# A hybrid decoder layer: the mLSTM's matmuls as three rounded passes, the local branch's weights rounded by casting transfers, and the gate rows' transpositions moved

## The chip, the cores and the metric

The kernel runs on one core of a Trainium2 chip. A core has a matrix engine (TensorE, PE), a vector engine (VectorE, DVE), a scalar engine (ScalarE, ACT), a general engine (GpSimd, POOL) and a synchronisation engine (SyncE, SP); SP and POOL issue most of the DMA transfers, each through a queue of its own. Every engine works through its own instructions in a fixed order and waits on semaphores where an input or a buffer isn't ready. On-chip memory has a large part (SBUF), with 128 partitions, and a small one (PSUM), into which PE writes its products.

The metric is the device time of one execution in microseconds (us), as a median of several executions.

## The reference

One decoder layer on a sequence of 512 tokens with 1024 channels. A normalised input feeds an mLSTM branch (4 heads, q and k of 128, v of 256 channels) and a sliding-window attention branch (16 query heads, 4 key heads of 64, window 128, with sinks). Each branch is multiplied by its weights and a sigmoid gate; the sum goes through an output projection, then come an MLP with squared ReLU, a gated per-layer embedding and a last norm. Everything is float32. Cut to the branches:

```python
proj = rmsnorm(x, norm_mix_g) @ w_in
qk_ml, v_ml, o_ml, if_pre, q_sw, k_sw, v_sw, g_a, g_b = split(proj)
qk_ml = silu(causal_depthwise_conv(qk_ml, conv_qk))
h_ml = mlstm_chunkwise(q_ml * ML_DQK ** -0.5, k_ml, v_ml, ig, lf)
h_ml = h_ml * rsqrt(mean(h_ml * h_ml) + EPS)
y_a = sigmoid(o_ml) * h_ml * mlstm_norm_g
y_b = swa_with_sinks(q_sw, k_sw, v_sw, sinks)
merged = sigmoid(g_a) * (y_a @ w_branch_a) + sigmoid(g_b) * (y_b @ w_branch_b)
x = x + merged @ w_out
```

The kernel computes the mLSTM without chunks, over the whole 512 x 512 lower triangle: for a head, scores k·q are multiplied by exp(log decay), and the result by v. The denominator is a row sum of the same weighted scores, which comes out of the same product through a column of ones beside v.

## The kernel before

**Arithmetic.** Most products are made of three passes in a rounded float32 format (F32R). An operand is split into a high part, the value rounded by a cast on ACT, and a low part, the rest, by a subtraction on DVE (`split`, L134). A product is then high·high + high·low + low·high (`pairs` L163, `chain` L169). Two products of the mLSTM are an exception: the scores (L819) and the output (L831) are plain float32 matmuls.

**Weights.** `load_w` (L155) loads 512 KB of weights through SP's queue into a raw buffer `wr` and splits it into `wh` and `wl`, each with four buffers (`WB`).

**v and the output gate.** `by_tokens` (L484) makes v (`w_vml`) and then the output gate (`w_o`) by seven half-size products instead of eight, through `seven` (L438): sums of weight quadrants are formed on DVE (L448 to L462), and the seven products are named p1, c11, t21, t22, c22, c12, c21. Each of them is two half products (one for each of two weight tiles) of 12 passes with 512 columns, 14 half products in all. p1 and c11 share a pair of PSUM banks (`pst`), so c11's first half product, the third of the 14, may start only when p1 has been copied out on ACT (L507); the first half product of t21, the fifth, writes another pair (`psg`). `put_v` (L517) writes v into the tiles `vm`, `put_o` (L582) takes the sigmoid and sends the gate to device memory (`god`).

**Gate rows.** Input and forget gates are made into rows of 4 x 512 on DVE (`mst`, a scan; `rr`, `gg`), and `em` is an exponential of `mst` on ACT (L562), whose table has to be loaded first. Between v and the output gate, 14 small transpositions on PE (L572, L574) turn `gg` and `em` into columns, and five DVE copies (L577, L578) bring them into `gc`.

**mLSTM and the local branch's weights.** After the attention come: the last q and k projection (`qk_proj(7)`), all eight SiLUs, then a loop over the four heads. Per head there are `ml_decay` (exponentials on ACT), `ml_scores`, `ml_out`, and one product of the local branch, `branch_b` (24 passes with 512 columns, eight of them in all), as work for PE while the other engines prepare the next head. The other four `branch_b` stand between the transpositions of the heads' results (`ya_of`).

**Order.** Each engine's order is set when the program is built: a scheduler places instructions from their dependences and program order; `issue_after` keeps a group behind a named matmul. Buffers are handed round in rings, so an instruction also waits for the last reader of the buffer that it writes.

Of the kernel before, what the change touches and what calls it, by code (L numbers as in the profile page):

```python
# [16 lines left out]
P = 128  # L17
# [19 lines left out]
def block_kernel(  # L37
# [82 lines left out]
    def tk(n):  # L120
        return tp_.tile([P, NH * (DV + 1)], F32, tag="tk", bufs=4, name=nm(n))

# [6 lines left out]
    def r32(t):  # L129
        return t.bitcast(F32)  # L130
# [348 lines left out]
    for m in range(NT):  # L479
        t = tk("vm").rearrange("p (h d) -> p h d", h=NH)  # L480
        G.memset(t[:, :, DV : DV + 1], 1.0)
        vm.append(t)

    def by_tokens(w, post, own_first=False):  # L484
# [81 lines left out]

    pgc = pg[:, :512]
    with tc.issue_after(last_mm[0].ins):
        for t in range(NT):
            for s in range(t + 1):  # L570
                c = (t * NT + s) * 4
                T.transpose(pgc[:, c : c + 4], gg[t][:, s * P : (s + 1) * P], ident[:4, :4])  # L572
            c = (NT * NT + t) * 4
            T.transpose(pgc[:, c : c + 4], em[:, t * P : (t + 1) * P], ident[:4, :4])  # L574
    gc = c1.tile([P, NT * NT + NT, 4], F32, name="gc")
    for t in range(NT):
        V.tensor_copy(gc[:, t * NT : t * NT + t + 1, :], pgc[:, t * NT * 4 : (t * NT + t + 1) * 4].rearrange("p (a b) -> p a b", b=4))  # L577
    V.tensor_copy(gc[:, NT * NT :, :], pgc[:, NT * NT * 4 : (NT * NT + NT) * 4].rearrange("p (a b) -> p a b", b=4))  # L578


    god = dp.tile([P, NH, NT, DV], F32, name="god")
# [9 lines left out]

    by_tokens(w_o, post_by_tokens(put_o))

# [178 lines left out]

    qk_proj(7)

    for h in range(NH):
        silu(h)
        silu(4 + h)


    hs = [[act_f("hs") for _ in range(2)] for _ in range(NH)]  # L780
# [7 lines left out]
    def ml_decay(h):  # L788
# [7 lines left out]
        )  # L796
        wT = []
        for s in range(NT):
            dm = act_f("dm")
            for t in range(s, NT):  # L800
                src = dg if t == s else pr
                A.activation(
                    dm[:, t * P : (t + 1) * P],
                    src[:, t * P : (t + 1) * P],
                    AF.Exp,
                    bias=gc[:, t * NT + s, h : h + 1],
                )
            wT.append(dm)
        wts[h] = wT

    def ml_scores(h):

        two, one = ps_a(), ps_t()
        banks = [two[:, :512], two[:, 512:], one, two[:, 512:]]
        at = [0, 0, 0, 384]
        for s in (0, 1, 3, 2):
            n0 = s * P
            psc = banks[s][:, at[s] : at[s] + S - n0]
            T.matmul(psc, qk[4 + h][:, n0 : n0 + P], qk[h][:, n0:], start=True, stop=True, skip_group_check=True)  # L819
        for s in range(NT):  # L820
            n0 = s * P
            dm = wts[h][s]
            V.tensor_mul(dm[:, n0:], banks[s][:, at[s] : at[s] + S - n0], dm[:, n0:])

    def ml_out(h):
        wT = wts.pop(h)
        for half in (1, 0):
            pn = ps_a().rearrange("p (n c) -> p n c", n=2)
            for t in (2 * half, 2 * half + 1):
                for s in range(t + 1):  # L830
                    last_mm[0] = T.matmul(  # L831
                        pn[:, t % 2, : DV + 1], wT[s][:, t * P : (t + 1) * P], vm[s][:, h, :], start=s == 0, stop=s == t, skip_group_check=True
                    )
            A.copy(hs[h][half].rearrange("p (n c) -> p n c", n=2), pn[:, :, :DV])
            V.tensor_copy(hd[:, h, 2 * half : 2 * half + 2], pn[:, :, DV])
# [24 lines left out]
    def branch_b(i):  # L860
        ps = ps_g()
        mm_T(ps, load_w(w_b[i], KT * P, KT), yb)
        t2[i] = act_f("gb")
        V.tensor_mul(t2[i], ps, gate_of(gbd, i))


    _, ya = big_hl("ya")

# [6 lines left out]

    ml_decay(0)
    ml_scores(0)
    rds = []
    for h in range(NH):
# [12 lines left out]
    for h in range(NH):  # L892
        branch_b(NH + h)
        ya_of(h)


# [541 lines left out]
```

## Time and profile before

| | |
|---|---|
| median of three runs | 880.56 us (880.06 to 881.1) |
| the profiled execution | 879.82 us, of which 878.0 us span |
| mean clock granted to PE | 0.998 |
| output gate's half products | from 83.45 us |
| mLSTM with the local branch's products | about 325 to 399.55 us |

The span is what the profile covers, from its first instruction to its last; the rest of an execution lies around it. The profile's page gives busy shares of the engines and the chain of waits that ended last; the views by window and the timeline of one engine show a stretch of the program. Names such as `psg<-x,wh` mean that a tile `psg` was written from `x` and `wh`; L171 is the line of the kernel. The lines themselves stand in the prediction, where they are used.

### The profile page before, as it was taken

The page shows a single profiled execution, that of the slowest core. Times are in us where ns is not written, and L with a number is a line of the kernel's source. Part 1 is how long each engine was busy: PE and PEld are TensorE (multiplying, and loading weights), DVE is VectorE, ACT ScalarE, POOL GpSimd, SP SyncE. Part 2 cuts the span into 40 slices and gives each one's busy share as a digit, 9 for nine tenths or more (in the row PEclk, how much of TensorE's full clock was granted, in tenths as well). Part 3 has the DMA queues.
Part 4 walks back from the last instruction along what each step waited for, and adds up shares of the span by engine and source line. Part 5 has one row for each costly group of instructions (what it writes and reads, how often), then busy time and mean ns, then how long its engine had stood idle before and what let it go on. Part 6 is the DMA issues. An engine that isn't in the chain of part 4 may idle for free.

```text
span 878.0 us, 11545 instructions
## 1 busy us (share of the span) xinstructions
PE 866.8 (99%) x4372; PEld 725.6 (83%) x4372; DVE 657.2 (75%) x966; ACT 483.5 (55%) x803; POOL 34.1 (4%) x58
## 2 busy tenths in 40 slices
PE   8999999999999999999999999999999999999996
PEld 7888889998777777788888888888888888888886
DVE  6999887875789876665896669756956794698557
ACT  6684554544676768743344665356435634564843
POOL 1111010000000000000020000000000000020000
PEclk9999999999999999999999999999999999999999
DMA  7765244435122162274244612530352054125302
GB/s 266 211 180 186 73 150 169 165 111 196 52 73 72 49 199 88 97 240 144 72 75 145 236 49 71 197 106 10 124 185 75 1 186 149 49 52 141 121 0 96
DMA packets 32793, 106.74 MB, mean 122 GB/s; under 512 B 4573, under 2 KB 4573, under 8 KB 32738
## 3 DMA queue, kind: packets, MB, share of 16 engines
q1 hardware_dynamic: 27570, 93.15, 31.2%
q0 software_dynamic: 5024, 12.59, 5.9%
q8 instruction: 34, 0.56, 0.3%
q10 hardware_dynamic: 144, 0.26, 0.1%
q14 instruction: 21, 0.17, 0.1%
HBM read 91.30 MB, written 8.40 MB: 114 GB/s over the span
## 4 chain that ended last, share of the span: by engine, by line
PE 90%; DVE 4%; ACT 3%; DMA 2%; issue 1%; SPq 0%; ACTq 0%; DVEq 0%
PE psg L171 50%; PE psp L171 23%; PE psa L171 7%; PE pst L171 4%; PE psa L831 1%; PE pst L747 1%; DVE wl L138 1%; DMA wr<-in_w_vsif 1%; ACT lm L712 1%; PE psa L819 1%; PE psa L689 1%; PE psa L690 1%; ACT wh L137 0%; DMA wr<-in_w_gb 0%; PE psp L980 0%
## 5 line engine op out<-in xcount | busy, mean ns | idle before, releaser
L137 ACT CAST wh<-wr 128x1024 fp32r<-128x1024 f32 x138 | 144.8, 1051 | 180.3 <-PE psg L171 74.8
L138 DVE TENSOR_TENSOR wl<-wr,wh 128x1024 fp32r<-128x1024 f32 x138 | 167.8, 1219 | 85.9 <-ACT wh L137 84.6
L171 PE MATMUL psg<-x,wh 128*128 128x512 f32 x512 | 157.7, 389 | 0.0
L171 PE MATMUL psp<-wh,uf 128*128 128x512 f32 x448 | 138.6, 389 | 0.0
L171 PEld LDWEIGHTS psg<-x,wh 128*128 128x128 f32 x512 | 96.0, 188 | 19.9
L171 PE MATMUL psg<-x,wl 128*128 128x512 f32 x256 | 99.6, 389 | 0.0
L171 PEld LDWEIGHTS psp<-wh,uf 128*128 128x128 f32 x448 | 84.1, 188 | 17.5
L171 PE MATMUL psp<-wl,uf 128*128 128x512 f32 x224 | 87.2, 389 | 0.0
L171 PE MATMUL psg<-h,wh 128*128 128x512 f32 x256 | 81.1, 395 | 0.7 <-DVE rc L715 0.7
L137 ACT CAST wh<-wd 128x1024 fp32r<-128x1024 f32 x44 | 46.2, 1052 | 54.0 <-PE psp L171 21.9
L138 DVE TENSOR_TENSOR wl<-wd,wh 128x1024 fp32r<-128x1024 f32 x44 | 53.1, 1217 | 14.7 <-ACT wh L137 14.5
L171 PEld LDWEIGHTS psg<-x,wl 128*128 128x128 f32 x256 | 48.0, 188 | 10.0
L171 PEld LDWEIGHTS psg<-h,wh 128*128 128x128 f32 x256 | 47.0, 188 | 11.2 <-issue 1.6
L171 PE MATMUL psg<-h,wl 128*128 128x512 f32 x128 | 50.5, 395 | 0.0
L138 DVE TENSOR_TENSOR uf<-F,uf 128x1792 fp32r<-128x1792 f32 (+2 forms) x20 | 33.0, 1652 | 21.8 <-ACT uf L137 21.8
L171 PEld LDWEIGHTS psp<-wl,uf 128*128 128x128 f32 x224 | 42.0, 188 | 8.7
L171 PE MATMUL psg<-yb,wh 128*128 128x512 f32 x128 | 41.3, 402 | 0.1
L171 PE MATMUL psg<-ya,wh 128*128 128x512 f32 x128 | 39.5, 390 | 0.0
L137 ACT CAST uf<-F 128x1792 fp32r<-128x1792 f32 (+2 forms) x20 | 27.9, 1396 | 20.5 <-DVE F L1133 20.4
L1157 DVE SCALAR_TENSOR_TENSOR xk<-psp,r,xk 128x512 f32<-128x512 f32 x48 | 33.7, 744 | 5.5 <-PE psp L171 5.2
L171 PE MATMUL psg<-hS,wh 128*128 128x256 f32 x192 | 35.6, 284 | 0.0
L171 PE MATMUL psa<-h,wh 128*128 128x256 f32 x192 | 35.3, 285 | 0.2 <-ACT p L625 0.2
(322 smaller groups left out, 1745.6 us busy)
## 6 DMA issues: line engine op xcount, KB each, us to landing
wr<-in_w_up SPq DMA_DIRECT2D x32, 512.0 KB, 3.3
wd<-in_w_down SPq DMA_DIRECT2D x24, 512.0 KB, 3.7
wr<-in_w_qsw SPq DMA_DIRECT2D x8, 512.0 KB, 4.3
gd<-gr POOLq DMA_DIRECT2D x8, 512.0 KB, 3.7
wr<-in_w_qkml SPq DMA_DIRECT2D x8, 512.0 KB, 3.2
wr<-in_w_b SPq DMA_DIRECT2D x8, 512.0 KB, 3.2
gl<-gd SPq DMA_DIRECT2D x8, 512.0 KB, 3.4
wr<-in_w_a SPq DMA_DIRECT2D x8, 512.0 KB, 4.4
```

What stands on the lines that cost most here:

```text
L137: A.copy(dst[0], src)
L138: last_low[0] = V.tensor_sub(dst[1], src, r32(dst[0]))
L171: last_mm[0] = T.matmul(ps, l, r, start=first and i == 0, stop=last and i == len(ops) - 1, skip_group_check=parts)
L689: T.matmul(o, q[:, n * P : (n + 1) * P], kk[kp][ab][:, k0 : k0 + 256], start=True, stop=False)
L690: T.matmul(o, q[:, n * P : (n + 1) * P], kl[kp][ab][:, k0 : k0 + 256], start=False, stop=True)
L712: A.activation(lm3[:, g, :], lm3[:, g, :], AF.Exp, bias=nmx[:, g : g + 1], scale=0.125, accum_out=sm[:, g : g + 1])
L747: T.matmul(o[HALF[ab], :], v[:, c : c + 64], w[:, ab * 512 : (ab + 1) * 512], start=j == 0, stop=j == len(terms) - 1)
L819: T.matmul(psc, qk[4 + h][:, n0 : n0 + P], qk[h][:, n0:], start=True, stop=True, skip_group_check=True)
L831: last_mm[0] = T.matmul(pn[:, t % 2, : DV + 1], wT[s][:, t * P : (t + 1) * P], vm[s][:, h, :], start=s == 0, stop=s == t, skip_group_check ...
L1157: V.scalar_tensor_tensor(o, ps[:, t, :], r2[:, 2 * toks + t : 2 * toks + t + 1], o, ALU.mult, ALU.add)
```

## The change

1. The mLSTM's scores and output become three rounded passes each. q and k of a head are split (`qk_parts`), as are the weighted scores (in pieces of 512, 384 and 384 columns), into tiles of `ya`, which isn't needed until later. The score pieces are kept without their empty left parts: for the last two key blocks both products have 256 columns.
2. v is stored rounded in `vm`, with two columns of ones a head. Its low part is made by a subtraction and sent to device memory (`vld`, eight writes through POOL's queue); `ml_out` reads it back (`vl`, 512 KB a head through SP's queue).
3. `branch_b`'s weights get their high part by a transfer from device memory that casts (POOL's queue) instead of the cast on ACT; the low part is still a subtraction on DVE, from the raw tile that SP's queue loads as before.
4. The gate rows' transpositions and the copies into `gc` move from before the output gate to after its product t21.
5. In the mLSTM stage `ml_decay(0)` and the buffers come ahead of `qk_proj(7)`; only head 0's SiLUs and split stand before the first scores; two `branch_b` stand before head 0's output, one before each later one, a further one before head 3's scores, and two instead of four are left for the transpositions of the results.

```diff
-    def load_w(src, n, dims, raw=None):
+    def load_w(src, n, dims, raw=None, cast=False):
...
-        split(parts, raw[:, :n])
+        if cast:
+            nc.gpsimd.dma_start(out=parts[0], in_=src)
+            last_low[0] = V.tensor_sub(parts[1], raw[:, :n], r32(parts[0]))
+        else:
+            split(parts, raw[:, :n])
...
     def put_v(m, nh, ps, k):
         o = vm[m][:, 2 * nh : 2 * nh + 2, :DV]
-        src = ps.rearrange("p (h d) -> p h d", h=2)
+        two = lambda t: t.rearrange("p (h d) -> p h d", h=2)
+        low = act_r("vl")
         if k is None:
-            A.copy(o, src)
+            A.copy(o, two(ps))
+            V.tensor_sub(two(low), two(ps), r32(o))
         else:
-            V.tensor_add(o, src, k.rearrange("p (h d) -> p h d", h=2))
+            V.tensor_add(k, ps, k)
+            A.copy(o, two(k))
+            V.tensor_sub(two(low), two(k), r32(o))
+        nc.gpsimd.dma_start(out=vld[:, 2 * nh : 2 * nh + 2, m, :], in_=two(r32(low)))
...
-    by_tokens(w_o, post_by_tokens(put_o))
+    post_o = post_by_tokens(put_o)
+
+    def post_gates(what, ps):
+        post_o(what, ps)
+        if what == "t21":
+            gate_columns()
+
+    by_tokens(w_o, post_gates)
...
+    def spare():
+
+        k = turn[0] % KT
+        turn[0] += 1
+        return [t[:, k, :] for t in ya_parts]
+
+    def qk_parts(h):
+        for i in (h, 4 + h):
+            hl = spare()
+            split(hl, qk[i])
+            qk[i] = hl
...
+        for s in range(NT):
+            n0 = min(s, 2) * P
+            ops = pairs([t[:, s * P : (s + 1) * P] for t in k], [t[:, n0:] for t in q])
+            for j, (l, r) in enumerate(ops):
+                T.matmul(psc[s], l, r, start=j == 0, stop=j == 2, skip_group_check=True)
+        dm, wT = wts[h]
+        hl = []
+        for j, n in enumerate((512, 384, 384)):
+            for s in ((0,), (1,), (2, 3))[j]:
+                V.tensor_mul(wT[s], psc[s][:, P:] if s == 3 else psc[s], wT[s])
+            hl.append([t[:, :n] for t in spare()])
+            split(hl[j], dm[j][:, :n])
...
+        low = sp.tile([P, NT, DV], F32R, tag="lm", bufs=LMB, name=nm("vl"))
+        nc.sync.dma_start(out=r32(low), in_=vld[:, h])
...
+                    T.matmul(o, hi, vm[s][:, h, :], start=s == 0, stop=False, skip_group_check=True)
+                    T.matmul(o[:, :DV], hi, low[:, s, :], start=False, stop=False, skip_group_check=True)
+                    last_mm[0] = T.matmul(o, lo, vm[s][:, h, :], start=False, stop=s == t, skip_group_check=True)
...
     ml_decay(0)
+    qk_proj(7)
+    silu(0)
+    silu(4)
+    qk_parts(0)
     ml_scores(0)
...
     for h in range(NH):
-        branch_b(h)
+        for _ in range(1 if h else 2):
+            branch_b(todo.pop(0))
         if h + 1 < NH:
             ml_decay(h + 1)
+            qk_parts(h + 1)
         with tc.issue_after(last_mm[0].ins):
             rds.append(ml_out(h))
         if h + 1 < NH:
+            if h == 2:
+                branch_b(todo.pop(0))
             with tc.issue_after(last_mm[0].ins):
                 ml_scores(h + 1)
...
     for h in range(NH):
-        branch_b(NH + h)
+        if h % 2 == 0:
+            branch_b(todo.pop(0))
         ya_of(h)
```

First place: ACT at the start of the output gate, before. The `p_` rows are the copies of p1 out of PSUM (`pst`), `wh` are weight casts, `em` the exponential of the gate rows, `sgo` the first sigmoids.

```order
L562 ACT_TABLE_LOAD
L562 ACTIVATE em_877<-mst_855 4x512
L137 CAST wh_969<-wr_916 128x1024
L137 CAST wh_985<-wr_918 128x1024
L137 CAST wh_1008<-wr_908 128x1024
L507 COPY p_184_961<-pst_925 128x512
L507 COPY p_185_963<-pst_926 128x512
L137 CAST wh_1026<-wr_910 128x1024
L586 ACT_TABLE_LOAD
L586 ACTIVATE sgo_1001<-pst_925 128x512
```

The same place with the change (L531 are v's new roundings, L572 is now `em`, L512 the copies of p1):

```order
L137 CAST wh_981<-wr_928 128x1024
L137 CAST wh_997<-wr_930 128x1024
L531 CAST vm_530<-t_134_711 128x2x256
L531 CAST vm_532<-t_135_713 128x2x256
L137 CAST wh_1020<-wr_920 128x1024
L137 CAST wh_1038<-wr_922 128x1024
L572 ACT_TABLE_LOAD
L572 ACTIVATE em_908<-mst_886 4x512
L512 COPY p_192_973<-pst_937 128x512
L512 COPY p_193_975<-pst_938 128x512
L582 ACT_TABLE_LOAD
L582 ACTIVATE sgo_1013<-pst_937 128x512
```

`em` with its table load has moved from ahead of three weight casts to directly ahead of the two copies, and the second cast of the fifth and sixth half products (`wh_1038`) now stands ahead of both too.

Second place: PE at the start of head 0's output products, before. `vm` is v, `dm` the weighted scores, `yb` the local branch's result.

```order
L171 MATMUL psg_3512<-yb_2985,wl_3516 128x512
L831 MATMUL psa_3476<-vm_530,dm_3401 128x257
L831 MATMUL psa_3476<-vm_532,dm_3406 128x257
L171 MATMUL psg_3615<-yb_2452,wh_3618 128x512
L171 MATMUL psg_3615<-yb_2453,wh_3618 128x512
L831 MATMUL psa_3476<-vm_534,dm_3410 128x257
```

And with the change, where `ya_3358` and `ya_3359` hold the high and low parts of the weighted scores:

```order
L175 MATMUL psg_3508<-yb_3016,wl_3512 128x512
L867 MATMUL psa_3562<-vm_530,ya_3358 128x258
L868 MATMUL psa_3562<-vl_3560,ya_3358 128x256
L869 MATMUL psa_3562<-vm_530,ya_3359 128x258
L867 MATMUL psa_3562<-vm_532,ya_3358 128x258
L868 MATMUL psa_3562<-vl_3560,ya_3358 128x256
```

Three passes stand where one matmul stood, behind the second `branch_b` and no longer the first.

Third place: DVE in the mLSTM stage with the change, at head 1's scores: the multiplications by the decay (L852), the low parts of the weighted scores (L138, `ya`), and the low part of the seventh `branch_b` weight (L162, `wl`, whose high part comes from the casting transfer).

```order
L852 TENSOR_TENSOR dm_3543<-psa_3608,dm_3543 128x512
L852 TENSOR_TENSOR dm_3544<-psa_3608,dm_3544 128x384
L138 TENSOR_TENSOR ya_3359<-dm_3545,ya_3358 128x384
L138 TENSOR_TENSOR ya_3359<-dm_3543,ya_3358 128x512
L900 TENSOR_TENSOR gb_3663<-psg_3632,gl_3664 128x512
L138 TENSOR_TENSOR ya_3359<-dm_3544,ya_3358 128x384
L819 TENSOR_TENSOR dg_3667<-row_912,tri 128x512
L162 TENSOR_TENSOR wl_4042<-wr_4039,wh_4041 128x1024
L852 TENSOR_TENSOR dm_3671<-pst_3735,dm_3671 128x256
```

Before, the weighted scores had no low parts; here are head 2's multiplications (L823) and what follows them:

```order
L823 TENSOR_TENSOR dm_3547<-psa_3587,dm_3547 128x512
L823 TENSOR_TENSOR dm_3552<-psa_3587,dm_3552 128x384
L823 TENSOR_TENSOR dm_3556<-pst_3588,dm_3556 128x256
L823 TENSOR_TENSOR dm_3559<-psa_3587,dm_3559 128x128
L285 RECIPROCAL rs_3599<-sd_3597 128x8
```

Three subtractions of low parts now stand behind a head's multiplications, and a weight's subtraction, which waits for a casting transfer, in front of the next head's.

More of the change, by code (lines that the diff above doesn't have):

```diff
@@ L565, in block_kernel @@
         nc.gpsimd.dma_start(out=rows[h], in_=rrd[h : h + 1, :].broadcast_to([P, 512]))
[L567 to L578, printed above, removed]
     god = dp.tile([P, NH, NT, DV], F32, name="god")
@@ L771, in block_kernel @@
             swa_out(*units[u][:2])
[L773 to L777, printed above, removed]
+    ya_parts, ya = big_hl("ya")
+    turn = [0]
+    def spare():
[7 more added lines that the diff above has]
+            qk[i] = hl
     hs = [[act_f("hs") for _ in range(2)] for _ in range(NH)]
@@ L796, in ml_decay @@
         )
-        wT = []
+        dm = [act_f("dm") for _ in range(3)]
+        wT = [dm[0], dm[1][:, :384], dm[2][:, :256], dm[2][:, 256:384]]
         for s in range(NT):
-            dm = act_f("dm")
             for t in range(s, NT):
```

49 lines of the change are left out of this document (29 added, 20 removed).

## The prediction, made before the change was run

> **What bounds the kernel now.** I read the page first: busy shares, the slices, and the chain that ended last.
>
> ```profile
> PE 866.8 (99%) x4372; PEld 725.6 (83%) x4372; DVE 657.2 (75%) x966; ACT 483.5 (55%) x803; POOL 34.1 (4%) x58
> ...
> PEclk9999999999999999999999999999999999999999
> ...
> PE 90%; DVE 4%; ACT 3%; DMA 2%; issue 1%; SPq 0%; ACTq 0%; DVEq 0%
> ```
>
> TensorE (PE) is busy for 866.8 of the span's 878.0 us at full clock, and nine tenths of the chain are matmuls. So a matmul that goes away is time gained one for one, and a microsecond for which PE waits is lost one for one: little idle time comes later to swallow it. Next, the chain in order of time (start, length, what) at the stages that the change touches.
>
> ```profile
> 77.05 5.44 PE psa L171 x24
> 83.45 11.11 PE pst L171 x48
> 94.56 10.88 PE psg L171 x48
> ...
> 136.58 2.88 PE psg L171 x24
> ...
> 324.48 0.69 PE psg L171 x2
> ...
> 332.23 1.72 PE psa L819 x6
> 333.95 0.43 PE pst L819 x2
> 334.38 4.58 PE psg L171 x20
> 338.97 0.87 PE psa L831 x4
> ...
> 340.29 3.47 PE psa L831 x16
> ```
>
> ```profile
> 393.22 5.46 PE psg L171 x24
> 398.68 0.87 PE pst L873 x8
> 399.55 6.59 PE psg L171 x29
> ```
>
> Matmuls are pipelined, so I price one by the interval between issues and not by its recorded length. A rounded pass of 512 columns costs 5.44/24 = 0.227 us, one of 256 columns 2.88/24 = 0.120 us. The output gate's half products, 12 passes each, run from 83.45 without a break. In the mLSTM one head's scores take 1.72 + 0.43 = 2.15 us, and its output products 0.87 + 3.47 = 4.34 us for 20 records (two for each full-precision matmul). That stage begins where the row at 324.48 ends, at about 325.1, and ends at 399.55 with the first merge.
>
> Then the engines' busy time by stretch; the columns are window, length, busy time of PE, of weight loads, of VectorE (DVE), of ScalarE (ACT), of POOL, clock and DMA.
>
> ```profile
> 78.00:88.00 10.00, 10.00 (x54) 8.16 (x53) 10.00 (x17) 5.25 (x7) 1.06 (x2) 1.00 0.31 95
> 88.00:98.00 10.00, 10.00 (x45) 8.28 (x45) 9.18 (x9) 6.96 (x9) 1.45 (x2) 1.00 0.13 54
> ```
>
> ```profile
> 325.00:345.00 20.00, 19.87 (x85) 15.45 (x84) 15.56 (x30) 18.07 (x39) 0.00 (x0) 1.00 0.38 134
> 345.00:365.00 20.00, 19.85 (x89) 15.91 (x87) 11.74 (x31) 16.10 (x43) 0.00 (x0) 1.00 0.28 90
> 365.00:385.00 20.00, 20.00 (x93) 16.37 (x92) 13.04 (x32) 11.82 (x27) 0.00 (x0) 1.00 0.68 234
> ```
>
> Around the start of the output gate neither PE nor DVE has any idle time until about 95 us: what is added to DVE there makes something late. In the mLSTM stage ACT is the fuller engine at first and DVE has room.
>
> **The change, part by part.**
>
> *mLSTM products in three passes.* Output: before 80 records x 4.34/20 = 17.4 us; after, 30 passes a head of 258 or 256 columns, 120 x 0.120 = 14.4 us: -3.0. Scores: before 4 x 2.15 = 8.6 us; after, each head has three passes of 512 columns, three of 384 and six of 256. No row has 384; between 0.120 and 0.227 I take the middle, 0.173, and either end moves the sum by 0.6 at most. So 4 x (0.681 + 0.519 + 0.72) = 7.7 us: -0.9. Less PE work, all of it on the path: **-3.9 us** (bounds -3.3 and -4.5).
>
> *Splits in that stage.* A head gets five more casts on ACT and five more subtractions on DVE, and ACT loses eight casts of weights. What they cost, by an elementwise DVE run, a weight subtraction and an ACT copy of the same size:
>
> ```profile
> 330.78 4.29 DVE L676 SCALAR_TENSOR_TENSOR acc<-acc,sg 128x512 f32<-128x512 f32 x7
> ```
>
> ```profile
> 342.66 0.56 ACT L834 COPY hs<-psa 128x512 f32<-128x512 f32 x1
> ```
>
> ```profile
> 325.19 1.05 ACT L137 CAST wh<-wr 128x1024 fp32r<-128x1024 f32 x1 [0.40 <-PE psg L171]
> ```
>
> A subtraction is 4.29/7 = 0.61 us: 20 of them are at most 12.3 us, against 19.7 us of DVE idle time in the three windows above. ACT gains 20 x 0.56 = 11.2 and loses 8 x 1.05 = 8.4 us, +2.8 against 14.0 idle. So the engines have room; what counts is when a piece is ready. I laid the changed order on these prices, with PE's rows between: head 0's scores wait about 0.3 us for the low parts of q and k, although one whole branch product now stands ahead as cover; head 1's output products wait about 0.9 us for the weighted scores' low parts; heads 0, 2 and 3 come out with little slack (0 to 1.7 us). Before, the stage lasts 74.4 us and its work is 8 x 5.46 (branch products) + 17.4 + 8.6 + 4 x 0.87 (transpositions) = 73.2, so it also holds 1.2 us of waits. Net **0**, bounds -1.2 (all hidden) and +1.5 (each of three tight heads half a microsecond late).
>
> *Casting transfers of the branch weights.* None is in the trace of before. The nearest rows are POOL's plain and accumulating transfers and SP's reads (KB each, median us to landing):
>
> ```profile
> gd<-gr POOLq DMA_DIRECT2D x8, 512.0 KB, 3.7
> hS<-s POOLq DMA_DIRECT2D x8, 256.0 KB, 4.4
> og<-god SPq DMA_DIRECT2D x4, 512.0 KB, 4.3
> xk<-q POOLq DMA_DIRECT2D x6, 256.0 KB, 5.5
> god<-t POOLq DMA_DIRECT2D x4, 256.0 KB, 2.7
> ```
>
> From 3.7 (same size, no arithmetic) to 11 (the accumulating 5.5 doubled for the size); I take 4.5, near the row of the same size, since a cast adds no second read. A transfer may start when the product four groups earlier has released its high-part buffer, and must have landed when DVE comes to its subtraction. In my laid-out order that leaves 6.5, 5.3, 7.2, 16, 12, 5.6, 3.0 and 6.4 us for the eight (estimates). Only the seventh is short at 4.5, by 1.5 us of DVE, and its product is far enough behind that PE doesn't notice: **0**. The cover goes at about 7 us, see the rivals. The added 4 MB of reads (8 x 512 KB) fall in windows with a DMA share of 0.28 to 0.68.
>
> *Low parts of v.* Eight subtractions of 0.61 us on DVE, 4.9 us, stand among the last products of v, and eight 256 KB writes on POOL's queue. ACT gets six casts. DVE being full, its scan and what hangs on it (the shared maximum `mst`, then `em`) come later: I get the scan's end at about 87.7. ACT's rows of before:
>
> ```profile
> 78.17 1.28 ACT L562 ACT_TABLE_LOAD   x1
> 79.56 0.63 ACT L562 ACTIVATE em<-mst 4x512 f32<-4x512 f32 x1
> ...
> 86.48 1.05 ACT L137 CAST wh<-wr 128x1024 fp32r<-128x1024 f32 x1 [2.86 <-PE pst L171]
> 87.85 0.59 ACT L507 COPY p<-pst 128x512 f32<-128x512 f32 x1 [0.32 <-PE pst L171]
> 89.16 0.59 ACT L507 COPY p<-pst 128x512 f32<-128x512 f32 x1 [0.72 <-PE pst L171]
> ```
>
> Before, `em` is done at 80 and the two copies of the first product out of PSUM follow PE at once; the third half product overwrites that PSUM, so it may start when the first copy is out. After, ACT's queue has two weight casts, the table load and `em` ahead of these copies (order, first place). The second of those casts writes the buffer that PE's second half product reads, so it starts only when that has ended, 82.5 + 24 x 0.227 = 87.9; then 1.05 (cast) + 1.28 (table) + 0.6 (`em`) + 0.59 (copy), 91.5, with a hand-over 91.7. PE has two matmuls of the fifth half product to fill with (0.45 us). Before, the third half product starts at 83.45 + 5.45 = 88.9 (24 passes). So +2.8 us at that point: an idle stretch of 3.3 us, of which 0.95 had been gained ahead of it. If a write of v's low parts (2.7 us in the row above) lands late, the copy waits for its buffer too; that adds 0 to 1.5.
>
> *Gate rows' transpositions.* They leave 82.42 to 83.38:
>
> ```profile
> 82.11 0.39 PE L171 MATMUL psa<-wh,h 128*128 128x512 f32 x1
> 82.42 0.22 PE L572 MATMUL psa<-ident,gg 4*128 4x4 f32 x1
> ...
> 83.38 0.50 PE L171 MATMUL pst<-wh,h 128*128 128x512 f32 x1
> ```
>
> The same 14 come back behind the sixth half product: 0.9 us there, partly counted in the 0.95 above, so the output gate is behind by 2.8 + 0.9 - 0.5 (some matmuls of the ninth that the order puts ahead and small waits of before) = 3.2. I take **+3.0** in all, bounds 0 and 6: nothing, if PE finds other work or the copy comes earlier than I think; 6, if the late write (1.5) and a slower clock (1.7, below) come on top. The one cover lost is DVE's: nothing else there can give way.
>
> *Sum.* -3.9 + 0 + 0 + 3.0 = -0.9 us. The profiled execution took 879.82 (span 878.0 and 1.8 around it), 0.74 under the median of the runs, 880.56. On the median's scale: 880.56 - 0.9 = about 879.7 us.
>
> **Rivals.**
>
> *A, the forecast: gain and stall nearly cancel.* 878.8 to 882.0, likeliest 879.7. Chance 0.42.
>
> *B, the third half product doesn't wait.* For it: the chain of casts, table and copy rests on my order of ACT's queue against PE's end; a wait on DVE that is shorter than I think lets `em` out early. Against it: the cast's buffer is read until 87.9 in any case, and the table load alone is 1.28. Then -3.9 + 0.5: 877.2, or 876 if the waits of 1.2 us in the mLSTM go too. Chance 0.30.
>
> *C, the idle stretch costs the clock too.* At the span's start, where PE had been idle, eight 128-column transpositions take 1.91 us, later four take 0.63:
>
> ```profile
> 7.95 1.91 PE L311 MATMUL pst<-ident,xn 128*128 128x128 f32 x8
> ...
> 12.98 1.22 PE L311 MATMUL psa<-ident,xn 128*128 128x128 f32 x8 [0.98 <-DVE xn L300]
> ...
> 17.64 0.63 PE L311 MATMUL pst<-ident,xn 128*128 128x128 f32 x4
> ```
>
> 0.24 against 0.16 us with the pipeline's tail in both, nearer to 2 to 1 without it. If 3.3 us of idling had that effect again, for as long as the start shows (7.7 to about 11 us), PE would lose half of some 3.4 us: +1.7, 881.4. Against it: the eight behind PE's idle 0.98 us, at 12.98, are not slow. Chance 0.08. The Trainium skill, "TensorE: Matmul & The Clock Gate", Part 1, says that the clock falls to half after an idle window of about 3.4 us and comes back after as much work; the stretch I forecast is just at that edge. By that rule the sum would be +0.8 and not -0.9.
>
> *D, the casting transfers are late: slower.* If they land in 8 us (between 3.7 and 11), the first, second, third, sixth, seventh and eighth are late by 1.5, 2.7, 0.8, 2.4, 5.0 and 1.6 us. DVE waits in order, and behind those waits stand the scores' products with the decay and their splits, which have no slack at heads 1 and 2. From about 7 us on PE waits; at 8 I count 4 us, at 9 about 8. 880.56 - 0.9 + 4 = 883.7. For it: the accumulating rows of half the size take 4.4 and 5.5. Against: the plain row of the same size. Chance 0.15.
>
> *E, the passes don't run at the rounded pace*, because weights change with each and 258 is no width that the trace has: 120 x 0.145 is the 17.4 us of before, and only the waits stay, 883. Against it: each of the 24 passes at 136.58 also loads new weights. Chance 0.05.
>
> **How the numbers follow.** What a measurement of this kernel can tell from no change is about 0.2%, 1.8 us: faster is below 878.8, slower above 882.3. B and a little of A lie below: 0.34. Most of A and half of C lie between: 0.41. D, E and the rest lie above: 0.25. Likeliest is A, 879.7, its own range 878.0 to 882.0. The range with the other cases: down to 876.3, which leaves out B's lower end, and up to 884.0, D at 8 us.
>
> **What would show it.** Right: the mLSTM's rows on L867 to L869 at 0.12 us each and the stage at 70.5 us instead of 74.4; one idle stretch of PE of about 3 us before the third half product, near 88 us, with `em` or the copy as releaser; the transpositions near 103. Wrong: no idle time there (B), slow matmuls behind it (C), DVE idle before the subtraction on L162 with DMA as releaser and PE idle behind it (D), passes of 0.145 us (E). An idle stretch anywhere else that is longer than 1 us, above all in the v projection from 60 to 82 us where DVE's added work begins, would be something that I haven't seen.

## The result, and the profile after

The changed kernel takes 883.03 us (median of 7 runs, 882.27 to 885.25) against 880.06 us (879.88 to 881.1) for the kernel before: a ratio of 1.0034, 95% interval 1.0022 to 1.0046. It is slower by 3.0 us; the forecast was 879.7 us and no measurable change. The profiled span grows from 878.0 to 881.3 us. Medians here and below are of the executions in the faster of two states; one execution, of the kernel without low parts, took 2198.87 us and isn't counted.

The page of the changed kernel, busy shares and chain:

```profile
PE 865.5 (98%) x4428; PEld 728.0 (83%) x4428; DVE 672.3 (76%) x994; ACT 489.2 (56%) x825; POOL 43.8 (5%) x70
...
PE 84%; DVE 7%; ACT 4%; DMA 2%; issue 2%; SPq 0%; ACTq 0%; DVEq 0%
```

PE is busy for only 1.3 us less, and its share of the chain falls from 90 to 84%: VectorE (DVE) and ScalarE (ACT) have taken over pieces of it. To find which, I compare the start of two groups of matmuls that exist in both kernels: the first product of the branch gates (behind the output gate) and the first behind the merge (behind the mLSTM). First the kernel before, from the chain and from PE's timeline:

```profile
125.76 3.14 PE psa L171 x24
```

```profile
448.74 5.75 PE psg L171 x24
```

Then the changed kernel, from the chain:

```profile
132.52 3.13 PE psa L175 x24
```

```profile
452.10 5.75 PE psg L175 x24
```

At the first mark the changed kernel is 6.8 us late, at the second 3.4, and at the end of the span 3.3. So the stretch between the marks, which holds the mLSTM, gains 3.4 us, much as forecast, and everything up to the branch gates loses 6.8, where 3.0 were forecast. The chain shows the place (start, length, what):

```profile
85.40 0.68 DVE t L530
86.08 1.13 DVE wr L453
87.22 1.20 DVE vl L532 x2
88.42 1.12 DVE mst L556
89.54 1.12 DVE wl L138
90.66 0.60 DVE rr L561
...
91.94 0.63 ACT em L572
92.57 0.47 ACT p L512
93.05 0.04 issue
93.09 7.34 PE pst L175 x24
100.43 4.99 PE psg L175 x22
```

Before, two rows of PE cover this stretch (from 83.45 and 94.56, in the prediction); now DVE and ACT carry it until 93.09, where the output gate's third half product starts. And the 24 passes of the third and fourth half products take 7.34 us instead of 24 x 0.227 = 5.45. PE's timeline has the wait, and ACT's shows what the third half product waited for:

```profile
93.09 0.50 PE L175 MATMUL pst<-wh,h 128*128 128x512 f32 x1 [4.20 <-ACT p L512]
```

```profile
86.64 1.05 ACT L137 CAST wh<-wr 128x1024 fp32r<-128x1024 f32 x1
88.52 1.05 ACT L137 CAST wh<-wr 128x1024 fp32r<-128x1024 f32 x1 [0.83 <-PE pst L175]
90.65 1.28 ACT L572 ACT_TABLE_LOAD   x1 [1.08 <-DMA vld<-vl]
91.94 0.63 ACT L572 ACTIVATE em<-mst 4x512 f32<-4x512 f32 x1
92.48 1.04 ACT L512 COPY p<-pst 128x512 f32<-128x512 f32 x2
```

The queue is the one in the prediction: two weight casts, table load, `em`, the copies. One wait had not been in it: the table load, and `em` behind it, stand for 1.08 us until a write of v's low part to device memory has landed. `em` takes over a buffer from which that write reads.

Two rows of DVE belong to it. `em` needs the scan `mst`, which stands at 88.42 in the chain above. The first row is the scan in the kernel before; the second, of the changed kernel, shows that DVE, without idle time there before, now stands idle for 1.41 us until a weight transfer has landed, ahead of the last low parts and the scan:

```profile
68.44 1.21 DVE L546 TENSOR_TENSOR_SCAN mst<-lf,ig 4x512 f32<-4x512 f32 x1
```

```profile
73.18 1.23 DVE L452 TENSOR_TENSOR wq<-wq,wq 128x1024 f32<-128x1024 f32 x1 [1.41 <-DMA wq<-in_w_o]
```

This wait differs between executions (0.58 and 0.71 us in the first two runs below), and all that follows it on DVE moves with it.

The granted clock explains the slow passes (window, length, busy time of PE, weight loads, DVE, ACT, POOL, then clock, DMA):

```profile
88.00:90.00 2.00, 0.89 (x4) 0.39 (x3) 2.00 (x3) 1.05 (x1) 1.42 (x2) 1.00 0.31 129
90.00:92.00 2.00, 0.00 (x0) 0.00 (x0) 2.00 (x7) 1.34 (x2) 0.44 (x1) 1.00 0.33 133
92.00:94.00 2.00, 0.91 (x4) 0.74 (x5) 2.00 (x6) 1.98 (x4) 0.50 (x2) 0.96 0.02 4
94.00:96.00 2.00, 2.00 (x6) 1.59 (x5) 2.00 (x2) 0.82 (x1) 1.75 (x4) 0.50 0.37 104
96.00:98.00 2.00, 2.00 (x7) 1.55 (x6) 2.00 (x3) 0.00 (x0) 0.00 (x0) 0.69 0.87 309
```

PE idles for 4.2 us, and less than a microsecond after it has come back its clock is 0.50, for 3.4 us. So the loss up to the branch gates is made of the late start (93.09 against 88.90, 4.2 us), the slow passes (7.34 - 5.45 = 1.9 us) and the transpositions, which are now paid behind the sixth half product (0.95 us), less 0.45 us for two passes of the fifth half product that PE did ahead of the wait: 6.6, with which PE leaves the output gate (117.50 against 110.89). At the mark it is 6.8, since a weight transfer between them took 4.14 instead of 3.99 us.

### The profile page after: what moved, and what is told of

Same layout as the page of the kernel before. It is cut to its first block, busy times and chain, and to the rows that moved or that the text cites. A ratio compares the mean times of both kernels' runs of the same rounds, so it can differ in the third digit from the quotient of the medians.

```text
span 881.3 us, 11733 instructions
## 1 busy us (share of the span) xinstructions
PE 865.5 (98%) x4428; PEld 728.0 (83%) x4428; DVE 672.3 (76%) x994; ACT 489.2 (56%) x825; POOL 43.8 (5%) x70
## 4 chain that ended last, share of the span: by engine, by line
PE 84%; DVE 7%; ACT 4%; DMA 2%; issue 2%; SPq 0%; ACTq 0%; DVEq 0%
PE psg L175 47%; PE psp L175 23%; PE psa L175 6%; PE pst L175 2%; DVE wl L138 2%; PE pst L766 1%; ACT wh L137 1%; DMA wq<-in_w_o 1%; DMA wr<-in_w_vsif 1%; ACT lm L731 1%; PE psa L708 1%; PE psa L847 1%; DVE qs L429 1%; PE psa L709 1%; DMA wr<-in_w_gb 0%
## 5 line engine op out<-in xcount | busy, mean ns | idle before, releaser
L137 ACT CAST wh<-wr 128x1024 fp32r<-128x1024 f32 x130 | 136.6, 1052 | 162.5 <-PE psg L175 60.3
L138 DVE TENSOR_TENSOR wl<-wr,wh 128x1024 fp32r<-128x1024 f32 x130 | 158.2, 1220 | 82.3 <-ACT wh L137 81.2
L138 DVE TENSOR_TENSOR wl<-wd,wh 128x1024 fp32r<-128x1024 f32 x44 | 53.1, 1219 | 14.6 <-ACT wh L137 14.5
L138 DVE TENSOR_TENSOR uf<-F,uf 128x1792 fp32r<-128x1792 f32 (+2 forms) x20 | 33.0, 1652 | 21.8 <-ACT uf L137 21.8
```

Of the source, the lines that this page charges most:

```text
L137: A.copy(dst[0], src)
L138: last_low[0] = V.tensor_sub(dst[1], src, r32(dst[0]))
```

## The experiments

The theory after this reading: the only loss is at the start of the output gate, its root is the work for v's low parts on DVE in a stretch where DVE has no idle time, and the path is DVE, then ACT's queue with its waits for buffers, then PE, whose clock falls. The rivals: the transpositions' new place, the casting transfers, or the mLSTM stage itself. Eleven kernels were run; each was timed beside the kernel before on the same chip, which took 880.0 to 880.1 us in every group.

**Does the idle stretch cost the clock?** 32 more matmuls, which nobody reads, in the idle stretch:

```diff
     def post_gates(what, ps):
         post_o(what, ps)
+        if what == "p1":
+            with tc.issue_after(last_mm[0].ins):
+                for i in range(32):
+                    T.matmul(pg[:, 512:768], A11[0][0][:, :P], A11[0][0], start=True, stop=True, skip_group_check=True)
```

> The changed kernel with 32 more matmuls of 256 columns on PE, whose result nobody reads, in the idle stretch ahead of the output gate's third half product (32 x 0.12 = 3.8 us of the 4.2 us). Theory (the idle stretch costs twice: as a wait, and because the clock falls to half behind it): the third half product still starts at about 93.1 us, but its first passes take 0.23 and not 0.43 us, so the time falls by about 1.9 us, from 883.0 to 881.1. Rival (the passes are slow because of something else that runs at 93 to 97 us, transfers or late low parts): passes and time unchanged, 883.0.

Measured: 882.27 us, ratio to the kernel before 1.0025 (1.0016 to 1.0034). PE's timeline:

```profile
88.26 3.99 PE L611 MATMUL psa<-h 128*128 128x256 f32 x32
92.24 0.50 PE L175 MATMUL pst<-wh,h 128*128 128x512 f32 x1
92.57 0.39 PE L175 MATMUL pst<-wl,h 128*128 128x512 f32 x1
92.80 0.63 PE L175 MATMUL pst<-wh,h 128*128 128x512 f32 x2
```

The passes behind it come at 0.23 us again (92.57, 92.80), so the clock is shown: a busy PE keeps it, and the 24 passes take 5.73 us and not 7.34. Yet the time falls by only 0.8 us by the medians, 0.9 by the spans (880.4 and 881.3). The half product also began 0.85 us earlier than in the changed kernel, and the filling isn't the reason: in this execution DVE waited 0.58 and not 1.41 us for its weights, and `em` 0.24 and not 1.08 us for the write. PE leaves the output gate 2.0 us earlier (115.50 against 117.50): 0.85 for the start, 1.6 for the passes, less 0.45 for the two passes that the filling displaced. At the branch gates (131.70 against 132.52) 0.8 us of it is left, because a weight transfer in the chain took longer, here first and then in the changed kernel:

```profile
117.97 5.33 DMA wr<-in_w_gb
```

```profile
119.97 4.14 DMA wr<-in_w_gb
```

Why it took longer isn't shown. The forecast of -1.9 was nearly right for the passes and wrong for the time.

**Does `em`'s buffer matter?** `em` goes into the tile of the log forget gates, which is free by then, and the four row tiles of the same ring are allotted after the output gate:

```diff
-    em = act_f("em")[:4, :]
+    em = lf
     A.activation(em, mst, AF.Exp, scale=-1.0)
-    rows = [row("row") for _ in range(NH)]
...
     by_tokens(w_o, post_gates)
+    rows = [row("row") for _ in range(NH)]
```

> The changed kernel with em written into the tile of the log forget gates, which is free by then, so that em no longer takes over a buffer of v's low parts and no longer waits for that buffer's write to device memory to land. Theory (em's table load waited 1.1 us for that landing, ACT's order did the rest): table load at about 88 and not 90.65, the copy of p1 then waits for the same landing behind one more weight cast, the third half product starts at about 91.9 and not 93.1: -1.2 us for the wait, and if an idle stretch of 3.2 us is too short to slow the clock, another -1.9: 880 to 882. Rival (the scan on VectorE at 89.5 sets it): start and time unchanged within 0.3 us, 883.0.

Measured: 879.69 us, ratio 1.0001 (0.9992 to 1.0011): by the medians the whole loss against the kernel before is gone, 3.3 us for one buffer. The ten executions fall into two groups: six of 879.1 to 879.9 us with a mean clock of 0.998 to 0.999, four of 881.2 to 882.0 with 0.994 to 0.996. The trace is of the first group. PE's timeline:

```profile
90.94 0.50 PE L175 MATMUL pst<-wh,h 128*128 128x512 f32 x1 [2.06 <-ACT p L512]
```

The third half product starts 2.1 us earlier. 1.2 were expected; 0.7 us came from DVE, which had waited 0.71 and not 1.41 us for its weights, so that the scan began at 87.61 and not 88.34. The idle stretch is 2.06 us, and the passes behind it are at full clock (1.00 from 92 us on). In this execution the edit takes away a wait and with it the half clock; the mean clocks of the slower four say that PE ran slowly for longer there, but not where. What is left of the wait now hangs on the scan: `em` waits 0.58 us for it, and one weight cast and the copies follow.

**Low parts formed in place.** The last six low parts overwrite the sum that they come from, and are sent from there.

```diff
-        low = act_r("vl")
+
+        def low_part(low, src):
+            V.tensor_sub(two(low), two(src), r32(o))
+            nc.gpsimd.dma_start(out=vld[:, 2 * nh : 2 * nh + 2, m, :], in_=two(low))
+
...
             V.tensor_add(k, ps, k)
             A.copy(o, two(k))
-            V.tensor_sub(two(low), two(k), r32(o))
-        nc.gpsimd.dma_start(out=vld[:, 2 * nh : 2 * nh + 2, m, :], in_=two(r32(low)))
+            low_part(k, k)
```

> The changed kernel with the low parts of v's last six pieces formed in place, in the buffer of the sum, and sent from there: as many subtractions and writes, six buffers fewer, and no wait of em or of the copies for the last writes. Theory (waits for buffers of the low parts): the third half product begins at about 89, is held once more by its weights' low part on VectorE until about 92, and the idle stretch is cut to pieces under 3 us: -2 to -3 us, 880 to 881. Rival (VectorE's added 4.9 us alone set the delay): the half product ends as late as now, at most -0.5 us.

Measured: 882.32 us, ratio 1.0023 (1.0014 to 1.0033), hardly better than the change. ACT's timeline:

```profile
88.42 0.59 ACT L512 COPY p<-pst 128x512 f32<-128x512 f32 x1
...
91.98 0.59 ACT L512 COPY p<-pst 128x512 f32<-128x512 f32 x1 [2.03 <-DMA vld<-t]
```

The first copy comes at 88.42 as hoped; the second waits 2.03 us for the landing of such a write, in another buffer. My expectation named DVE as the next limit and missed that fewer buffers only move the wait to the next one in line. The scan, however, is back at 69.30, though all eight subtractions are still on DVE. The clock fell here too (0.50 at 93 to 95 us), although the longest idle stretch was 1.88 us:

```profile
89.06 0.49 PE L175 MATMUL pst<-wh,h 128*128 128x512 f32 x1 [0.64 <-ACT p L512]
90.01 0.73 PE L175 MATMUL psg<-wh,hS 128*128 128x512 f32 x2 [0.45 <-ACT wh L137]
92.62 0.79 PE L175 MATMUL pst<-wh,h 128*128 128x512 f32 x1 [1.88 <-ACT p L512]
```

Three short stretches with three matmuls between them went with the half clock that 4.2 us in one piece had brought.

**The same, with the subtractions after product t21.**

```diff
+            later.append(lambda: low_part(k, k))
...
         if what == "t21":
             gate_columns()
+            for f in later:
+                f()
```

> As the run before, but the subtractions of these six low parts and their writes are put behind the output gate's product t21, where VectorE has idle time. Theory (the loss is VectorE's added work in a stretch where it is full, and what queues behind it): the stall at 88 to 93 us, the half clock behind it and the late start go, about -5.5 to -6.3 us against the changed kernel: 876.7 to 877.5, faster than the kernel before by 3. Rival (the loss comes from the transpositions' new place or the extra transfers): no more than -1 us.

Measured: 887.23 us, ratio 1.0078 (1.0061 to 1.0095): a plain miss. From PE's and ACT's timelines:

```profile
101.79 0.27 PE L604 MATMUL psa<-ident,em 4*128 4x4 f32 x1 [5.13 <-ACT em L577]
```

```profile
99.81 1.28 ACT L577 ACT_TABLE_LOAD   x1 [2.18 <-DMA vld<-p]
```

`em` had again been given a buffer of a low part, whose write now came later still, and the transpositions waited 5.13 us for it, which PE has to run ahead of other work. The run doesn't test DVE's load, since the wait that it was to take away had only been moved.

**No low parts at all**, with the number of passes kept:

```diff
-            V.tensor_sub(two(low), two(k), r32(o))
-        nc.gpsimd.dma_start(out=vld[:, 2 * nh : 2 * nh + 2, m, :], in_=two(r32(low)))
...
-                    T.matmul(o[:, :DV], hi, low[:, s, :], start=False, stop=False, skip_group_check=True)
+                    T.matmul(o[:, :DV], hi, vm[s][:, h, :DV], start=False, stop=False, skip_group_check=True)
```

> The changed kernel without v's low parts: no subtractions, no writes to device memory, no reads back; the pass of the mLSTM output that multiplies the low part takes the high part once more, so that the number and width of the passes stay (v's low part is left out of the result). Theory (the low parts' work on VectorE, their writes and what waits for them cause the whole loss of 6.7 us at the output gate, the rest of the change gains 3.4): 876.5 to 877.5 us, 3 us faster than the kernel before. Rival (the moved transpositions or the casting transfers share in the loss): above 878.5.

Measured: 876.72 us, ratio 0.9958 (0.9941 to 0.9975). This settles that the low parts are the root: without their subtractions, writes, reads and buffers, the rest of the change, its moved transpositions and casting transfers included, gains 3.3 us. It doesn't say which of the four it is. The first pass of the branch gates starts at 126.06 (before: 125.76).

**Casts on ACT again** (`cast=True` taken out of `branch_b`):

> The changed kernel with the local branch's weights cast on ScalarE again, as before, and no casting transfers. Theory (the transfers land in time, the one wait of 2.0 us on VectorE costs PE nothing): 883.0 within 0.5 us, or slightly slower because ScalarE gets 8.4 us of casts back. Rival (the transfers are late and cost the 0.5 us that the mLSTM stage gained less than forecast): 882.5 or less.

Measured: 883.22 us, ratio 1.0033 (1.002 to 1.0046), the time of the changed kernel. The casting transfers neither gain nor lose anything that can be measured. Their landing times and the one wait for them in the changed kernel:

```profile
wh<-in_w_b POOLq DMA_DIRECT2D x8, 512.0 KB, 3.7
```

```profile
359.93 1.22 DVE L162 TENSOR_TENSOR wl<-wr,wh 128x1024 fp32r<-128x1024 f32 x1 [2.04 <-DMA wh<-in_w_b]
```

**The casting transfers alone, on the kernel before** (its `branch_b` with the changed `load_w`):

> The kernel before with the casting transfers for the local branch's weights and nothing else. Theory (neutral: ScalarE loses 8.4 us off the path, the transfers land in about 3.7 us): 880.0 within 0.7 us. Rival (late transfers): 882 or more.

Measured: 880.88 us, ratio 1.0009 (1.0 to 1.0018). At most a little slower, not the 2 us of the rival.

**The moved transpositions alone, on the kernel before:**

> The kernel before with the gate rows' transpositions and copies behind the output gate's product t21 and nothing else. Theory (14 transpositions cost 0.95 us of PE wherever they stand, VectorE's five copies have room): 880.0 within 0.5 us. Rival (their place costs or gains by itself): more than 0.7 us either way.

Measured: 880.09 us, ratio 0.9999 (0.999 to 1.0009). Their place costs nothing.

**Gate rows' later work behind the sixth weights, transpositions behind t22, low parts in place, `em` in the free tile:**

```diff
+        if what == "c11":
+            row_work()
-        if what == "t21":
+        if what == "t22":
             gate_columns()
```

> The changed kernel with three edits: v's last six low parts formed in place; em written into the tile of the log forget gates; the gate rows' work behind the scan (rr, gg) placed behind the low parts of the output gate's fifth and sixth weights, the transpositions behind product t22. Theory (the start of the third half product is set by the copy of p1 on ScalarE and by its own weights' low part on VectorE): the copy is out at about 88, the weights' low part at about 89.5, the idle stretch under 1.5 us, the clock full; 877 to 878 us. Rival (a write of a low part still holds the copy, as in the run with parts formed in place): 880 to 882.

Measured: 879.15 us, ratio 0.9987 (0.9978 to 0.9997). The copies come at 87.92 and 89.18 on ACT and PE waits only 0.34 us for the weights' low part, as the theory has it. But it waits again at 101.63, 0.39 us for a weight cast that the later row work had pushed back, and smaller waits follow; the gain is less than the one forecast. All eight subtractions are still on DVE in the crowded stretch here, yet the kernel is 3.9 us faster than the changed one.

**Six of the eight subtractions on POOL:**

```diff
-            V.tensor_sub(two(low), two(k), r32(o))
+            G.tensor_sub(two(low), two(k), r32(o))
```

> As the run before, but with separate buffers for the low parts and six of the eight subtractions on GpSimd, so that VectorE has the load of before in this stretch. Theory (VectorE's added work is the root): the weights' low part is out before 88, the third half product starts without a wait at 88: 876.6 to 877.5 us. Rival (GpSimd's subtractions take several us each, or hold the buffers that the copy of p1 takes over): the wait comes back at the copy, 880 or more.

Measured: 888.96 us, ratio 1.0099 (1.0082 to 1.0116). POOL takes 1.2 us for a piece, not several, but it slows DVE, see the last section; the copies waited as well. The scan is late (92.04) although DVE has only two of the subtractions left.

**Low parts made after the read back.** v itself goes to device memory, and its rounded value is subtracted in the attention and mLSTM stages, where DVE has room; `em` is in the free tile.

```diff
-            V.tensor_sub(two(low), two(k), r32(o))
-        nc.gpsimd.dma_start(out=vld[:, 2 * nh : 2 * nh + 2, m, :], in_=two(r32(low)))
+        nc.gpsimd.dma_start(out=vld[:, 2 * nh : 2 * nh + 2, m, :], in_=two(k))
...
+    def ml_low(h):
+        low = sp.tile([P, NT, DV], F32R, tag="lm", bufs=LMB, name=nm("vl"))
+        nc.sync.dma_start(out=r32(low), in_=vld[:, h])
+        for m in range(NT):
+            V.tensor_sub(low[:, m, :], r32(low)[:, m, :], r32(vm[m])[:, h, :DV])
+        lows[h] = low
```

> The changed kernel with v's low parts made later: v itself goes to device memory, and the subtraction of its rounded value (four pieces of 256 columns a head) is done on VectorE after the read back, ahead of the head's output products; em is written into the tile of the log forget gates. VectorE has the load of before at 70 to 90 us, and 16 x 0.35 = 5.6 us more during the attention and the mLSTM. Theory (only VectorE's added work at the v projection and what queues behind it ate the gain): no stall at 88 us, the mLSTM stage gains 3 to 3.4: 876.7 to 877.5, faster than the kernel before by 0.3 to 0.4%. Rival (the subtractions delay the mLSTM's tight heads 1 and 2): the stage loses 1 to 2 of it, 878 to 879.

Measured: 877.65 us, ratio 0.9969 (0.9958 to 0.998), against 880.11 us: faster than the kernel before by 2.5 us and than the changed kernel by some 5. The stretch that used to stall, by window, and ACT's timeline:

```profile
88.00:92.00 4.00, 4.00 (x20) 3.26 (x19) 4.00 (x5) 1.61 (x3) 0.00 (x0) 1.00 0.11 44
```

```profile
87.50 0.58 ACT L512 COPY p<-pst 128x512 f32<-128x512 f32 x1
88.54 0.59 ACT L512 COPY p<-pst 128x512 f32<-128x512 f32 x1 [0.47 <-ACT p L512]
```

PE is busy throughout, the copies are out by 89.1, and the branch gates start at 126.36. The same passes and products are computed. The edit has three parts, though: `em` has the free tile, the low parts take two buffers of the ring and not eight, and the subtractions (16 of 0.42 us) stand later. The first alone gave 3.3 us (879.69), so 2.0 are left for the other two. The kernel keeps three quarters of what the run without low parts shows to be there.

**Buffers or DVE's load?** The scan tells them apart. In the five kernels with eight buffers of their own for the low parts (the changed one, the filling, `em` in the free tile, casts on ACT, subtractions on POOL) it starts between 87.49 and 92.04. In the five with two or none (in place, after t21, rows late, after the read back, no low parts) it starts between 68.54 and 70.01, as in the kernel before (68.44). In place it is early with all the subtractions on DVE, on POOL it is late with two of them there. So its late place goes with the buffers and not with DVE's load. What the load alone costs no run shows: the kernel with the subtractions in place and the rows late, 1.5 us slower than the one with them after the read back, differs in more than their place.

## Why the prediction was wrong, point by point

- **PE saturated, so that work taken away is time gained.** Right for the mLSTM stage, and for the lost time up to the end of the output gate. Behind it a weight transfer sets the start of the branch gates: in the run with the filling, PE was 2.0 us earlier ahead of it and 0.8 behind it.
- **mLSTM products in three passes, -3.9 us, with the stage's waits unchanged.** Right in kind, 0.5 too large: the stage gained 3.4 us (6.8 late at its first mark, 3.4 at its last). The passes run at the price taken, 0.12 us in the chain at 345 to 349 us, one row as an example, and the last head's scores take 1.92 us (376.73 to 378.65), as in the sum. So the 0.5 us are in the stage's waits: by the prediction's own sum 1.7 us instead of 1.2.

```profile
345.07 0.12 PE psa L867
```

- **Casting transfers, 0.** Right: they land in 3.7 us where 4.5 was taken, the seventh is the one that DVE waits for (2.04 us, 1.5 forecast), and neither their removal nor their addition alone moves the median by more than 0.1% (the interval of the addition goes up to 0.18%). Rival D, 883.7 us, came near the time and has the wrong cause.
- **Transpositions, 0.9 us wherever they stand.** Right.
- **v's low parts and ACT's queue, +3.0 us.** This is the step that failed, by size: place, order and direction are as forecast, and PE left the output gate 6.6 us late. Two things were missing in the term. First, the sum had `em` run as soon as the second weight cast was done; the trace shows it held for 1.08 us by the landing of a write, because `em` was given a buffer of a low part. I had counted that wait for the copies only and set it to "0 to 1.5" beside the sum. The cast itself began at 88.52 and not at 87.9, and the half product at 93.09 and not at 91.7. Second, the idle stretch came to 4.2 us and not 3.3, and cost 1.9 us of clock, which the sum had at nothing. The rest of the term held: transpositions less passes done ahead were 0.5 us, against 0.9 - 0.5.
- **DVE is full, so its scan comes later.** The scan did come late (its end at 89.55, 87.7 forecast), and the reason given for it is wrong: as the runs above show, its place goes with the buffers of the low parts, and DVE stood idle for 1.41 us ahead of it.
- **Rival C, the clock, 0.08.** It happened, on top of A, and at the price forecast (1.7 against 1.9 us of slow passes). I held the absence of slow rows behind a 0.98 us stretch against it, which says nothing of a stretch four times as long; in the trace with casts on ACT the same eight transpositions at 12.98, behind 1.34 us of idle time, take 1.81 and not 1.22 us, and the clock is 0.50 from 14 to 16 us. The Trainium skill's page "TensorE: Matmul & The Clock Gate", Part 1, gives an idle window of about 3.4 us as the point from which the clock is halved. The changed kernel agrees (4.2 us idle, half clock), but as a limit for a single stretch the figure isn't borne out: 2.56 us halved it in the run with the subtractions on POOL (last section).
- **Rival B, no wait at the third half product, 877.2 us.** Wrong for the changed kernel, but the runs without the low parts (876.72) and with them later (877.65) are that case.

The range, 876.3 to 884.0, held the time, but by luck: its upper end belonged to rival D, and the range of case A, 878.0 to 882.0, didn't hold it. The late write and the clock stood in the term as bounds, as two mishaps that might come on top ("6, if the late write (1.5) and a slower clock (1.7, below) come on top"). Both came, and the 6.6 us are a little over that bound. They aren't independent, since the late write lengthens the stretch in which the clock falls. Whether 3.3 us alone would have cost the clock no run shows; but 2.56 us did in the run with the subtractions on POOL, so the clock belonged in the sum.

## What to carry to other kernels

When work is added to an engine that is full in a stretch, ask which buffers its results occupy and for how long a write from them takes to land: whoever is given those buffers next waits for the landing, and that may be a small instruction that stands ahead of an important one. Buffers can also change where an instruction stands in its engine's order: here the scan came 20 us later with them. A wait that is long enough for PE's clock to fall costs more than its length, so two harmless looking delays in one place have to be added up before the second price is judged. Give a small result on the path a buffer that is free: `em` in another tile brought 3.3 us. Work that isn't needed before a later stage may stand there, even if its operand is at hand now: the low parts made after the read back, with that tile, turned a loss of 3.0 us into a gain of 2.5.

## What the runs showed of the hardware

The length of the longest idle stretch doesn't settle whether PE's clock is halved: 0.64, 0.45 and 1.88 us with three matmuls in between went with it, one of 2.06 us didn't, and one of 2.56 us, in the run with the subtractions on POOL, did. There the clock falls while PE still stands idle; PE's timeline, then a window, in which the clock is the third number from the end (0.66 in this half microsecond, 1.00 before it, 0.50 behind it):

```profile
91.00 0.79 PE L175 MATMUL pst<-wh,h 128*128 128x512 f32 x1 [2.56 <-ACT p L512]
```

```profile
90.50:91.00 0.50, 0.00 (x1) 0.00 (x1) 0.50 (x1) 0.48 (x2) 0.50 (x1) 0.66 0.00 0
```

It also differs between executions at a place that no edit touches: at 14 to 16 us the clock is 0.50 in the traces of four kernels (casts on ACT, rows late, after t21, casting transfers alone) and 1.00 in those of the other nine.

POOL and DVE slow each other. In the run with the subtractions on POOL, DVE's timeline and POOL's:

```profile
88.79 1.21 DVE L138 TENSOR_TENSOR wl<-wr,wh 128x1024 fp32r<-128x1024 f32 x1
89.92 2.20 DVE L462 TENSOR_TENSOR wr<-wr,wr 128x1024 f32<-128x1024 f32 x1
92.04 2.33 DVE L556 TENSOR_TENSOR_SCAN mst<-lf,ig 4x512 f32<-4x512 f32 x1
```

```profile
89.01 2.03 POOL L532 TENSOR_TENSOR vl<-t,vm 128x512 fp32r<-128x512 f32 x1 [3.68 <-ACT vm L531]
92.09 1.20 POOL L532 TENSOR_TENSOR vl<-t,vm 128x512 fp32r<-128x512 f32 x1
```

A DVE subtraction of two tiles in on-chip memory, 1.21 us by itself, takes 2.20 beside a POOL subtraction, the scan 2.33 instead of 1.21, and POOL's own piece 2.03 instead of 1.20: about as long as if one waited for the other. The Trainium skill, "SBUF — State Buffer", section "Who interferes with whom", says that a DVE instruction with two inputs in SBUF contends with a GpSimd instruction that reads SBUF, and calls the ports that they share an exclusive lock; these rows agree.
